# Reading back the diagonal blocks of a triangular inverse in four transfers of 8 rows

## The chip, the cores and the metric

The kernel runs on one core of a Trainium2 chip. The metric is device time in microseconds (us) of one execution, as the median of several runs. Besides that there is one profiled execution, recorded by the hardware profiler; all rows below come from it. Its engines are TensorE (PE for matmuls, PEld for weight loads), VectorE (DVE), ScalarE (ACT), GpSimd (POOL) and SyncE (SP). In this kernel SP issues every DMA. Each engine runs its own list of instructions strictly in order.

## The reference, cut to what matters

A two-layer model on 512 tokens of width 1024. Each layer is a gated feed-forward block, a mixer, and a second feed-forward block. The mixer joins three branches by gates: retention, a sparse attention, and RWKV-7, which is a recurrence over tokens:

```python
def step(S, inp):
    r_t, w_t, k_t, v_t, kk_t, a_t = inp
    sa = jnp.einsum('bhvk,bhk->bhv', S, -kk_t)
    S = S * w_t[:, :, None, :] + sa[..., None] * (kk_t * a_t)[:, :, None, :] + v_t[..., None] * k_t[:, :, None, :]
    return S, jnp.einsum('bhvk,bhk->bhv', S, r_t)
```

## The kernel before

**Staging.** `hybrid` runs, per layer, `ffn`, `mixer`, `ffn`. Nearly all PE time is spent in dense products with float32 weights, written as three passes each (L109, L111, L113, output `psd`). The weights are loaded in 256 KB pieces into `raw` (L54, four buffers), and ACT and DVE split each piece into a rounded part `whi` (L49) and a rest `wlo` (L50), three buffers each.

**The recurrence.** Class `Rwkv` handles the 8 heads as 4 pairs (`p` = 0 to 3 in `pairs`). Time is cut into 8 chunks of 64 tokens. `front2` and `mid` prepare a pair, `chain` walks its 8 chunks, `post` finishes it. Within a chunk the recurrence becomes a product with the inverse of a 64 by 64 unit triangular matrix, and `mid` computes these inverses. So there are 8 runs of `mid` in the program, 4 per layer; below they are called the first to eighth inverse.

**The inverse.** `nb` (tile tag `kh`) holds the strict triangles. Its 32 by 32 diagonal blocks, two per chunk and head, are written to a DRAM buffer `dn` in four DMAs (L480). One DMA then reads `dn` back into the tile `N` (tag `bk`, L481): 128 partitions by 32 rows by 32 numbers, the same 32 blocks copied to four groups of 32 partitions, 512 KB in all. The access pattern's outermost dimension is these four copies. After that, POOL runs a forward substitution over rows `u` = 0 to 30. Each row is two instructions, a product into a scratch tile `E` (L490) and a sum into `X` (tag `cum`, L492). Row `u` of the loop reads row `u` of `N` and nothing else of it. The result goes through DRAM once more: out by `dx<-cum` (L497), back into `mt` (L503). Two rounds of small matmuls (L510, L517) then join the blocks.

**Pacing.** After every fourth row, and after the last, PE gets a tiny matmul that reads `X` (L494, the pace). The program calls `fill` behind each pace to place a counted number of dense matmuls (`FP`, `FD`), so PE has work while POOL runs the next rows. While an inverse is under way, other branches' work is mixed in on POOL: `kd` and `m` of retention (L636, L631), `o` (L700), the softmax scaling `L` of the attention (L862), and `uv` of the chain (L542). A scheduler sets the order on each engine, from its own estimate of when each operand will be there. A changed estimate moves instructions on all engines.

**Waits.** SP reaches the read-back when the four writes to `dn` are done. POOL reaches its first row and waits for the read-back. Everything queued behind on POOL waits too.

Of the kernel before, what the change touches and what calls it, by code (L numbers as in the profile page):

```python
# [232 lines left out]
class Rwkv:  # L233
# [198 lines left out]
    def mid(self, d):  # L432

        nc, K, c = self.nc, self.K, self.cst
        st, bk, v = d["st"], d["bk"], d["v"]
        zo, nb = self.zo, self.t("kh", [P, 8, 64])
        for q in range(2):
            for h in range(2):
                s = slice(64 * h, 64 * h + 64)
# [12 lines left out]
        with self.tc.issue_after(zl.ins):  # L452
# [12 lines left out]
            for h in range(2):  # L465
                o = slice(64 - 64 * h, 128 - 64 * h)
                for par in range(2):
                    src = pv4[64 * par:64 * par + 64, :, h, :]
# [6 lines left out]
        dn = K.dram([4, 8, 32, 32], "dn", 2)  # L475
        N = self.t("bk", [P, 32, 32])
        for h in range(2):
            for b in range(2):
                src = nb[64 * h + 32 * b:64 * h + 32 * b + 32, :, 32 * b:32 * b + 32]
                nc.sync.dma_start(dn[2 * h + b].rearrange("c s t -> s c t"), src)  # L480
        nc.sync.dma_start(N, dn.rearrange("b c s t -> (b c) s t")[None].to_broadcast([4, 32, 32, 32]))  # L481

        X = self.t("cum", [P, 8, 32])
        tmp = self.t("E", [P, 8 * 31])
# [673 lines left out]
```

## Time and profile before

| | us |
|---|---|
| median of 3 runs | 3042.56 (3041.69 to 3042.8) |
| the profiled execution, its own time | 3045.66 |
| span in the profile, first to last instruction | 3043.9 |
| PE busy | 2908.3 (96% of the span) |
| DVE, ACT, POOL busy | 1741.9, 1082.4, 736.7 |

The span is read from the page's first lines. A time taken from a row is a time in the profiled execution, which took 3.1 us more than the median. In a timeline row the first number is the start in us from the span's beginning, the second the length. A bracket at the end says how long the engine stood idle just before and what ended that.

### The profile page before, as it was taken

Reading aid. Unit: us, or ns where it says so; the run is one execution under the profiler, and the core shown is the slowest. Engines: PE = TensorE matmul, PEld = TensorE weight load, DVE = VectorE, ACT = ScalarE, POOL = GpSimd, SP = SyncE. Lnnn points to the kernel's source line nnn. Section 1 sums busy time; section 2 is a strip of 40 time slices with the busy share of each in tenths; the row PEclk is TensorE's granted clock in tenths of the full one; section 3 lists DMA queues with packets and bytes.
Section 4 is the critical chain, followed back from the end, with each engine's and each line's share of the span. In section 5 each row is a group of like instructions: output and inputs, shape, how many; then the busy total and the mean of one; then the engine's idle time right before and its main releaser. Section 6 shows DMA issues by size and latency. Waiting matters only on the chain.

```text
span 3043.9 us, 39972 instructions
## 1 busy us (share of the span) xinstructions
PE 2908.3 (96%) x13968; PEld 2378.0 (78%) x13968; DVE 1741.9 (57%) x3694; ACT 1082.4 (36%) x1900; POOL 736.7 (24%) x1206
## 2 busy tenths in 40 slices
PE   9999999899899999999999999998988999999998
PEld 7888887777777778888888888777777777788886
DVE  5443378949674564444354433888485836644433
ACT  4333343244443233333333333533344432433322
POOL 2110124353433031110011101343534321311100
PEclk9999999999999999999999999999999999999999
DMA  4333322122324442333323334221323244423332
GB/s 137 97 97 104 112 92 73 63 88 81 94 84 148 131 153 94 97 97 95 100 94 97 97 107 118 83 71 60 95 74 97 92 143 132 145 94 97 97 97 87
DMA packets 198970, 305.66 MB, mean 100 GB/s; under 512 B 45808, under 2 KB 59888, under 8 KB 198768
## 3 DMA queue, kind: packets, MB, share of 16 engines
q1 hardware_dynamic: 198768, 303.10, 32.7%
q8 instruction: 110, 1.80, 0.3%
q14 instruction: 92, 0.75, 0.1%
HBM read 273.66 MB, written 29.36 MB: 100 GB/s over the span
## 4 chain that ended last, share of the span: by engine, by line
PE 73%; DVE 10%; POOL 7%; DMA 6%; issue 3%; ACT 1%; SPq 0%; DVEq 0%; POOLq 0%; ACTq 0%
PE psd L109 22%; PE psd L113 22%; PE psd L111 22%; POOL cum L492 3%; POOL E L490 2%; DMA bk<-dn 2%; DVE wlo L50 2%; DMA dx<-cum 1%; PE psr L444 1%; PE psr L533 1%; DMA th<-th 1%; PE psf L96 1%; DMA y<-y 1%; PE psr L558 1%; PE psr L96 1%
## 5 line engine op out<-in xcount | busy, mean ns | idle before, releaser
L49 ACT ACTIVATE whi<-raw 128x512 fp32r<-128x512 f32 (+2 forms) x920 | 571.3, 622 | 1300.8 <-PE psd L111 1002.6
L50 DVE TENSOR_TENSOR wlo<-raw,whi 128x512 fp32r<-128x512 f32 (+2 forms) x920 | 646.3, 703 | 552.7 <-ACT whi L49 545.4
L109 PE MATMUL psd<-xh,whi 128*128 128x512 f32 x2144 | 853.5, 398 | 1.5 <-DVE g L203 1.5
L111 PE MATMUL psd<-xl,whi 128*128 128x512 f32 x2144 | 848.9, 396 | 2.2 <-DVE xl L161 2.2
L113 PE MATMUL psd<-xh,wlo 128*128 128x512 f32 x2144 | 849.2, 396 | 0.1
L111 PEld LDWEIGHTS psd<-xl,whi 128*128 128x128 f32 x2144 | 408.1, 190 | 87.2 <-DVE xl L161 4.3
L113 PEld LDWEIGHTS psd<-xh,wlo 128*128 128x128 f32 x2144 | 408.0, 190 | 84.8 <-issue 0.7
L109 PEld LDWEIGHTS psd<-xh,whi 128*128 128x128 f32 x2144 | 408.5, 191 | 83.3 <-DVE g L203 1.7
L207 POOL TENSOR_TENSOR u<-s,u 128x512 f32<-128x512 f32 x88 | 140.9, 1602 | 841.6 <-DVE u L206 745.3
L109 PE MATMUL psd<-ah,whi 128*128 128x512 f32 x704 | 277.4, 394 | 0.0
L113 PE MATMUL psd<-ah,wlo 128*128 128x512 f32 x704 | 276.0, 392 | 0.0
L111 PE MATMUL psd<-al,whi 128*128 128x512 f32 x704 | 273.2, 388 | 0.0
L172 POOL TENSOR_TENSOR sq<-sq,sq 128x512 f32<-128x512 f32 x42 | 56.4, 1342 | 466.0 <-ACT sq L170 466.0
L111 PE MATMUL psd<-wlo,xh 128*128 128x512 f32 (+1 forms) x384 | 159.2, 415 | 0.0
L113 PEld LDWEIGHTS psd<-ah,wlo 128*128 128x128 f32 x704 | 132.1, 188 | 31.0
L111 PEld LDWEIGHTS psd<-al,whi 128*128 128x128 f32 x704 | 132.2, 188 | 29.6
L113 PE MATMUL psd<-whi,xl 128*128 128x512 f32 (+1 forms) x384 | 154.8, 404 | 0.0
L109 PEld LDWEIGHTS psd<-ah,whi 128*128 128x128 f32 x704 | 132.3, 188 | 26.3
L50 DVE TENSOR_TENSOR al<-u,ah 128x512 fp32r<-128x512 f32 x88 | 61.8, 702 | 153.6 <-ACT ah L49 153.6
L109 PE MATMUL psd<-whi,xh 128*128 128x512 f32 (+1 forms) x384 | 149.7, 410 | 0.0
L206 DVE TENSOR_TENSOR u<-psd,rb 128x512 f32<-128x512 f32 x88 | 60.9, 692 | 127.6 <-PE psd L113 127.6
L49 ACT ACTIVATE ah<-u 128x512 fp32r<-128x512 f32 x88 | 55.6, 632 | 169.4 <-POOL u L207 169.2
(305 smaller groups left out, 3946.6 us busy)
## 6 DMA issues: line engine op xcount, KB each, us to landing
raw<-in_wf_dram SPq DMA_DIRECT2D x184, 256.0 KB, 2.6
raw<-in_ffa_in_dram SPq DMA_DIRECT2D x176, 256.0 KB, 2.6
raw<-in_ffb_in_dram SPq DMA_DIRECT2D x176, 256.0 KB, 2.6
th<-th SPq DMA_DIRECT2D x96, 256.0 KB, 3.3
raw<-in_ffa_out_dram SPq DMA_DIRECT2D x80, 256.0 KB, 2.7
raw<-in_wt_dram SPq DMA_DIRECT2D x80, 256.0 KB, 2.8
raw<-in_ffb_out_dram SPq DMA_DIRECT2D x80, 256.0 KB, 2.6
x<-x SPq DMA_DIRECT2D x32, 256.0 KB, 4.4
```

Of the source, the lines that this page charges most:

```text
L49: self.nc.scalar.activation(hi, x, AF.Copy)
L50: self.nc.vector.tensor_tensor(out=lo, in0=x, in1=hi.bitcast(F32), op=ALU.subtract)
L96: return self.nc.tensor.transpose(out, x, self.ident)
L109: nc.tensor.matmul(out, ah, bh, start=start, stop=False)
L111: nc.tensor.matmul(out, ah, bl, start=False, stop=False)
L113: nc.tensor.matmul(out, al, bh, start=False, stop=stop)
L172: nc.gpsimd.tensor_tensor(out=sq, in0=sq, in1=self.ssq[0], op=ALU.add)
L206: nc.vector.tensor_tensor(out=u, in0=pu, in1=self.rb, op=ALU.mult)
L207: nc.gpsimd.tensor_tensor(out=u, in0=s, in1=u, op=ALU.mult)
L444: zl = nc.tensor.matmul(z[:, i * P:(i + 1) * P], bk[s, ck, :], st[h][s, ck, :], start=True, stop=True)
L490: nc.gpsimd.tensor_tensor(out=tv, in0=X[:, 0:n, u:u + 1].to_broadcast([P, n, w]), in1=N[:, u:u + 1, u + 1:].to_broadcast([P, n, w]), op=AL ...
L492: nc.gpsimd.tensor_tensor(out=X[:, 0:n, u + 1:], in0=X[:, 0:n, u + 1:], in1=tv, op=ALU.add)
```

## The change

The one read-back of 32 rows becomes four read-backs of 8 rows each. They read the same `dn`, write the same `N`, and keep the four copies outermost. Each moves 128 KB, a 1 KB piece per partition instead of one of 4 KB. The program issues them in order of `u`.

```diff
-        nc.sync.dma_start(N, dn.rearrange("b c s t -> (b c) s t")[None].to_broadcast([4, 32, 32, 32]))
+        for u in range(0, 32, 8):
+            src = dn.rearrange("b c s t -> (b c) s t")[:, u:u + 8, :]
+            nc.sync.dma_start(N[:, u:u + 8, :], src[None].to_broadcast([4, 32, 8, 32]))
```

The line numbers behind it grow by two, so L490 becomes L492. The built programs differ beyond the four DMAs, because the scheduler now expects the first rows earlier. At each place the order before is shown first, and then the order now. A bracket `[waits ...]` names what an instruction waits for; `DMAHW0` to `DMAHW7` are the eight counters that DMAs take in turn.

POOL, layer 0, first inverse. `E`, `cum`, `bk` belong to the inverse, `kd`, `m` to retention, `uv` to the chain. Before:

```order
L636 TENSOR_TENSOR kd_3824<-X_4091,kdec 128x128 [waits DVE_49]
L631 TENSOR_TENSOR m_4101<-X_4099,rss 128x4x32 [waits Activation_49,Pool_49]
L631 TENSOR_TENSOR m_4101<-X_4099,rss 128x4x32
L490 TENSOR_TENSOR E_4328<-cum_4327,bk_4321 128x31 [waits DMAHW7_49,DMAHW5_49]
L542 COPY uv_4835<-sv_989_4251 64x64 [waits Activation_49,Pool_49]
L542 COPY uv_4885<-sv_989_4251 64x64 [waits Activation_49]
L542 COPY uv_4835<-sv_990_4252 64x64 [waits Activation_49]
L492 TENSOR_TENSOR cum_4327<-cum_4327,E_4328 128x31 [waits Pool_49]
L542 COPY uv_4885<-sv_990_4252 64x64 [waits Activation_49]
L636 TENSOR_TENSOR kd_3824<-X_4099,kdec 128x128 [waits DVE_49]
```

Now:

```order
L492 TENSOR_TENSOR E_4331<-cum_4330,bk_4321 128x31 [waits DMAHW7_49,DMAHW5_49]
L494 TENSOR_TENSOR cum_4330<-cum_4330,E_4331 128x31 [waits Pool_49]
L638 TENSOR_TENSOR kd_3824<-X_4091,kdec 128x128 [waits DVE_49]
L633 TENSOR_TENSOR m_4101<-X_4099,rss 128x4x32 [waits Activation_49]
L492 TENSOR_TENSOR E_4331<-cum_4330,bk_4321 128x30 [waits Pool_49]
L633 TENSOR_TENSOR m_4101<-X_4099,rss 128x4x32
L544 COPY uv_4838<-sv_989_4251 64x64 [waits Activation_49,Pool_49]
L544 COPY uv_4888<-sv_989_4251 64x64 [waits Activation_49]
L494 TENSOR_TENSOR cum_4330<-cum_4330,E_4331 128x30 [waits Pool_49]
L544 COPY uv_4838<-sv_990_4252 64x64 [waits Activation_49]
L544 COPY uv_4888<-sv_990_4252 64x64 [waits Activation_49]
L492 TENSOR_TENSOR E_4331<-cum_4330,bk_4321 128x29 [waits Pool_49]
```

The first row of the inverse moved ahead of one `kd` and one pair of `m`, which now stand behind it.

POOL, same inverse, at rows 7 and 8 of the loop. Before:

```order
L490 TENSOR_TENSOR E_4328<-cum_4327,bk_4321 128x48 [waits Pool_49]
L492 TENSOR_TENSOR cum_4327<-cum_4327,E_4328 128x2x24 [waits Pool_49]
L490 TENSOR_TENSOR E_4328<-cum_4327,bk_4321 128x69 [waits Pool_49]
L492 TENSOR_TENSOR cum_4327<-cum_4327,E_4328 128x3x23 [waits Pool_49]
L490 TENSOR_TENSOR E_4328<-cum_4327,bk_4321 128x66 [waits Pool_49]
```

Now:

```order
L492 TENSOR_TENSOR E_4331<-cum_4330,bk_4321 128x48 [waits Pool_49]
L494 TENSOR_TENSOR cum_4330<-cum_4330,E_4331 128x2x24 [waits Pool_49]
L492 TENSOR_TENSOR E_4331<-cum_4330,bk_4321 128x69 [waits DMAHW0_49,Pool_49]
L494 TENSOR_TENSOR cum_4330<-cum_4330,E_4331 128x3x23 [waits Pool_49]
L492 TENSOR_TENSOR E_4331<-cum_4330,bk_4321 128x66 [waits Pool_49]
```

No instruction moved here. Row 8 (`128x69`) got a wait of its own on the second transfer's counter; rows 16 and 24 got the like.

SP, layer 0, second inverse: the writes to `dn`, the read-back, weight loads (`raw`) and two stores of the retention's output (`y<-sT`). Before:

```order
L54 DMA raw_5679<-in_wt_dram 128x512
L480 DMA dn_5797<-kh_5614 32x8x32 x4
L54 DMA raw_5705<-in_wt_dram 128x512
L481 DMA bk_5798<-dn_5797 128x1x1024
L54 DMA raw_5752<-in_wt_dram 128x512
L54 DMA raw_5770<-in_wt_dram 128x512
L978 DMA y_4_654_3052<-sT_5199 128x512
L978 DMA y_5_655_3053<-sT_5208 128x512
```

Now:

```order
L54 DMA raw_5682<-in_wt_dram 128x512
L480 DMA dn_5800<-kh_5617 32x8x32 x2
L54 DMA raw_5708<-in_wt_dram 128x512
L54 DMA raw_5755<-in_wt_dram 128x512
L480 DMA dn_5800<-kh_5617 32x8x32 x2
L54 DMA raw_5773<-in_wt_dram 128x512
L980 DMA y_4_654_3052<-sT_5202 128x512
L483 DMA bk_5801<-dn_5800 128x1x256 x4
L980 DMA y_5_655_3053<-sT_5211 128x512
```

Here two more weight loads and one store stand ahead of the read-back. On SP the read-back keeps its neighbours at the seven other inverses.

## Rows read from the trace of the kernel before

**Rows 1.** The page's first part: the span, then busy time, share of the span and instructions of each engine.

```profile
span 3043.9 us, 39972 instructions
PE 2908.3 (96%) x13968; PEld 2378.0 (78%) x13968; DVE 1741.9 (57%) x3694; ACT 1082.4 (36%) x1900; POOL 736.7 (24%) x1206
```

**Rows 2.** Who waited for whom over the whole program: total us, times, longest us.

```profile
POOL E L490 <- DMA bk<-dn: 98.4, 8, 28.6
...
PE psr L494 <- POOL cum L492: 24.8, 20, 5.7
...
PE psr L510 <- DVE m L504: 12.0, 14, 2.4
```

**Rows 3.** PE's timeline at the eight inverses: the first PE instruction that waited for POOL in each (start, length, ..., in the bracket the idle time before it and what ended it).

```profile
476.51 0.70 PE L652 MATMUL psf<-X,kd 128*64 128x128 f32 x4 [3.25 <-POOL kd L636]
...
631.45 0.33 PE L652 MATMUL psf<-X,kd 128*64 128x128 f32 x2 [0.52 <-POOL kd L636]
...
802.42 0.38 PE L494 MATMUL psr<-cum,ident 128*128 128x1 f32 x2 [4.69 <-POOL cum L492]
...
946.64 0.38 PE L494 MATMUL psr<-cum,ident 128*128 128x1 f32 x2 [1.98 <-POOL cum L492]
...
1980.88 0.48 PE L652 MATMUL psf<-X,kd 128*64 128x128 f32 x2 [3.10 <-POOL kd L636]
...
2143.44 0.38 PE L494 MATMUL psr<-cum,ident 128*128 128x1 f32 x2 [2.54 <-POOL cum L492]
...
2311.93 0.37 PE L494 MATMUL psr<-cum,ident 128*128 128x1 f32 x1 [5.75 <-POOL cum L492]
...
2457.40 0.38 PE L494 MATMUL psr<-cum,ident 128*128 128x1 f32 x2 [3.38 <-POOL cum L492]
```

**Rows 4.** Busy time in the 7 us that follow each of the longer waits of rows 3 (the window, its length, then us and instructions of PE, PEld, DVE, ACT and POOL, PE's granted clock, DMA share, GB/s).

```profile
476.51:483.51 7.00, 7.00 (x23) 5.42 (x24) 6.10 (x20) 1.78 (x4) 5.98 (x18) 0.60 0.12 37
802.42:809.42 7.00, 7.00 (x27) 5.88 (x28) 1.84 (x6) 1.18 (x3) 5.64 (x18) 0.76 0.00 1
...
1980.88:1987.88 7.00, 7.00 (x28) 5.53 (x29) 6.10 (x20) 2.17 (x5) 5.98 (x18) 0.78 0.10 37
2143.44:2150.44 7.00, 7.00 (x28) 5.70 (x29) 0.81 (x2) 1.86 (x3) 5.91 (x16) 0.76 0.12 39
2311.93:2318.93 7.00, 7.00 (x21) 5.95 (x22) 1.15 (x4) 1.01 (x2) 5.64 (x18) 0.53 0.00 0
2457.40:2464.40 7.00, 7.00 (x26) 5.67 (x27) 1.43 (x3) 1.27 (x3) 5.64 (x18) 0.76 0.13 37
```

**Rows 5.** The chain of work that ended last, in order of time (start, us, what): the read-backs on it, from issue to POOL's release, and after the first of them one transfer of 128 KB out of SBUF (`dx<-cum`) that also has four groups outermost.

```profile
463.96 10.62 DMA bk<-dn
...
504.43 4.74 DMA dx<-cum
...
787.42 11.21 DMA bk<-dn
...
933.47 9.19 DMA bk<-dn
...
1968.48 10.46 DMA bk<-dn
...
2129.74 10.81 DMA bk<-dn
...
2296.36 11.78 DMA bk<-dn
...
2443.83 10.07 DMA bk<-dn
```

**Rows 6.** POOL's timeline at the first, second and sixth inverse.

```profile
474.72 0.24 POOL L490 TENSOR_TENSOR E<-cum,bk 128x31 f32<-128x31 f32 x1 [7.05 <-DMA bk<-dn]
...
476.07 0.39 POOL L636 TENSOR_TENSOR kd<-X,kdec 128x128 f32<-128x128 f32 x1
476.43 0.86 POOL L631 TENSOR_TENSOR m<-X,rss 128x128 f32<-128x128 f32 x2
...
627.30 0.24 POOL L490 TENSOR_TENSOR E<-cum,bk 128x31 f32<-128x31 f32 x1 [4.97 <-DMA bk<-dn]
...
2140.69 0.24 POOL L490 TENSOR_TENSOR E<-cum,bk 128x31 f32<-128x31 f32 x1 [5.62 <-DMA bk<-dn]
```

**Rows 7.** SP's timeline at the first and second inverse: when the read-back, the weight load behind it and the store were issued (the length is that of the issue).

```profile
463.96 0.68 SPq L481 DMA_DIRECT2D bk<-dn  x1
464.75 0.38 SPq L54 DMA_DIRECT2D raw<-in_wt_dram  x1
...
617.22 0.55 SPq L481 DMA_DIRECT2D bk<-dn  x1
...
624.71 0.33 SPq L978 DMA_DIRECT2D y<-sT  x1
```

**Rows 8.** DMA issues: KB each and median us from issue to landing. The first row is of the whole program (a constant of 1 KB per partition), the second of the stretch 463 to 480 us alone.

```profile
cum<-in_idg_dram SPq DMA_DIRECT2D x8, 128.0 KB, 2.0
...
raw<-in_wt_dram SPq DMA_DIRECT2D x2, 256.0 KB, 10.3
```

**Rows 9.** Busy time, clock, DMA share of the 16 engines and GB/s (columns as in rows 4) in two us in which the read-back of the first inverse was under way; and ACT's timeline at the split of the weights that were loaded right behind it (the piece issued at 464.75).

```profile
468.00:470.00 2.00, 2.00 (x11) 1.64 (x10) 2.00 (x7) 0.73 (x2) 0.00 (x0) 1.00 0.25 72
...
484.28 0.63 ACT L49 ACTIVATE whi<-raw 128x512 fp32r<-128x512 f32 x1 [1.06 <-PE psd L113]
```

## The prediction

> **What bounds the kernel now.** I read the page's first part, then the waits, then PE's timeline. PE is busy for 2908.3 of 3043.9 us [rows 1], so time can only be saved where PE stands idle or runs at its lower clock. The table of waits leads to the place: POOL stood 98.4 us, eight times, before the first row of an inverse until the read-back landed, and PE stood 24.8 us at the paces that POOL releases [rows 2]. Most of POOL's 98.4 us costs nothing, because PE had other work meanwhile. What counts is PE's own idle time. In all eight inverses the first PE instruction that waited for POOL stands shortly after the read-back's landing, and the idle times before it are 3.25, 0.52, 4.69, 1.98, 3.10, 2.54, 5.75 and 3.38 us, 25.2 us in all [rows 3]. In the first and fifth the wait is for `kd`, which is queued on POOL behind the inverse's first row; in six inverses it is at a pace or again at `kd`.
>
> A second loss follows the idle time. In the 7 us after it the granted clock was 0.60, 0.76, 0.78, 0.76, 0.53 and 0.76 of full speed in six of the eight inverses, although PE was busy throughout [rows 4]. So a part of each stretch ran at the lower of the two levels (1.2 instead of 2.4 GHz). The work lost is 7 us times one minus the clock: 2.8, 1.7, 1.5, 1.7, 3.3 and 1.7 us, 12.7 us in all. I count none for the second and fourth inverse.
>
> Idle time and clock loss together are what PE can win back, inverse by inverse: 6.05, 0.5, 6.4, 2.0, 4.6, 4.2, 9.05 and 5.1 us. I call these the stakes. Their sum is 37.9 us.
>
> **When the first 8 rows land.** The read-back took 9.19 to 11.78 us from issue to POOL's release [rows 5]. While the first was under way alone, the DMA share was 0.25 and the rate 72 GB/s [rows 9]. That is four engines of 16, and at 72 GB/s the 512 KB take 7.3 us. A transfer of 128 KB that also has four groups outermost took 4.74 us [rows 5]. From 4.74 at 128 KB to 10.62 at 512 KB is 5.9 us for 393,000 bytes, or 67 GB/s, close to the 72. So I read a fixed part of about 3 us and a part that grows with the bytes. The first quarter should land 4.7 us after its issue. The bounds are 2.0 us, the landing of a 128 KB constant with the same 1 KB per partition [rows 8], and 10.6 us, no earlier than the whole. I take 4.7 because that row has the same size and the same outermost dimension. The later quarters follow at the queue's rate and are not waited for: POOL needs 3.4 to 3.8 us or more for the rows of each quarter (14 to 16 instructions, of which the first took 0.24 us [rows 6]), against some 2 us of transfer.
>
> The Trainium skill, "DMA: Bandwidth & Descriptors", section "Anatomy of one DMA", gives each DMA about 2.0 us of fixed cost plus its bytes at 436 GB/s. By that 128 KB would take 2.3 us, all stakes would be won, and the sum would be 37.9 us. The same page's rules advise joining small transfers, which speaks against this change, and by the same formula the whole read-back would take only 3.2 us. The trace has 10.62.
>
> **The change part by part.** *The earlier first row.* Without anything else, POOL's first row would start 10.62 less 4.7, or 5.9 us earlier in the first inverse. From the other rows of rows 5 it is 6.5, 4.5, 5.8, 6.1, 7.1 and 5.4 us in the third to eighth.
>
> *POOL's order.* In the first and fifth inverse one `kd` (0.39 us) and two `m` (0.86 us) that ran before the first row now run after it [rows 6]. They must still be done before the first pace, so 1.3 us of the lead are lost: 4.6 and 4.5 us remain. In the sixth, `kd` and `m` also fall behind the first row, which leaves 4.8; POOL is free for it early enough, as it had waited 5.62 us there [rows 6].
>
> *What PE gets.* PE gains the smaller of stake and lead. First inverse 4.6 (of 6.05), third 6.4 (the stake), fourth 2.0 (the stake), fifth 4.5 (of 4.6), sixth 4.2 (the stake), seventh 7.1 (of 9.05), eighth 5.1 (the stake). The sum is 33.9 us. Where the lead is the smaller, POOL is the next to be late: its 31 rows then set the pace from the first to the last.
>
> *The second inverse* I put at zero. Its stake is 0.5, and SP now reaches the read-back only behind a store. That store was issued at 624.71, the read-back at 617.22 [rows 7]. At worst the quarter lands at 624.7 plus 4.7, so the first row comes 2.1 us later than at 627.30 [rows 6]. At best the store comes earlier too, and the lead covers the stake.
>
> *Three more issues on SP.* At 0.55 to 0.68 us each [rows 7] they hold the queue for about 2.0 us. The next weight load stands behind them. It was issued at 464.75 and landed 10.3 us later [rows 7, 8], at 475.05, so it was itself held by the read-back's bytes, which stay the same. ACT splits this piece at 484.28 [rows 9]. The margin of 9.2 us falls to 4.6 as PE comes earlier, and still covers 2.0. Cost zero; without that cover it would be 2.0 us per inverse.
>
> *Everything else that moved.* Some hundred instructions change places with neighbours, mostly in layer 0 between the first and second inverse. They compute the same and PE stays the bound. I have no row for their sum, and bound it by the one class of waits that lies behind each inverse, PE waiting at L510 for the returned inverse: 12.0 us in all [rows 2]. I allow half of it, 6 us, either way, and take zero, because leads and delays can both come of it.
>
> **The sum.** The profiled execution took 3045.66 us, and 33.9 less is 3011.8. It ran 3.1 us above the median of the runs, so against the median of 3042.56 the forecast is 3008.7, about 3009 us, 1.1% faster. With the first quarter at 2.0 us all stakes are won: 3004.7. With the 6 us either way, 2999 to 3015.
>
> **The rivals.** *First: a transfer's time is mostly fixed, so a quarter lands not much before the whole.* If it takes 7.7 us, each lead shrinks by 3.0, and the gains are 1.6, 0, 3.5, 1.5, 1.5, 1.8, 4.1 and 2.4, or 16.4 us: 3026 us. The 2.0 us of rows 8 speak against it; for it speaks that no row shows a read of this shape at this size. The Trainium skill's fixed cost, in the page and section named above, is of this kind: 2.0 of the 2.3 us it gives a quarter. Chance 0.13.
>
> *Second: the four transfers share the four engines and land together, and the kernel is slower.* Then the first row waits for all 512 KB and for three issues more, 2.0 us longer than now. In the first and fifth inverse `kd` and `m`, which now stand behind that row, come 1.3 us later still. That is 2.0 us in six inverses and 3.3 in two, 18.6 us: about 3061 us. It turns into a loss where the first quarter lands later than some 9.3 us after its issue. Against it: the weight load issued 0.8 us behind the read-back landed at 475.05, after POOL was released at 474.58 (463.96 plus 10.62) [rows 5, 7, 8]. A load that shared the engines evenly with a transfer twice its size would have been done before. The queue seems to serve in order. Chance 0.07.
>
> *Third: the lead is won at the first row and lost by the last.* POOL's rows share their engine with `L`, `o`, `kd` of other branches. If these now fall between rows, the paces wait instead of the first row, and half the gain goes: 3026 us. For it speaks that the 24.8 us at the paces came in 20 waits, so late rows do reach PE [rows 2]. Against it, that 18.3 of these 24.8 us are the first paces of five inverses [rows 3]. Chance 0.08.
>
> That the rows still wait for all four transfers is ruled out by the built order: the first row waits for one counter, and row 8 for another.
>
> **How the numbers follow.** Forecast 0.72, first rival 0.13, third 0.08, second 0.07. The range is 2999 to 3027: it takes in the early landing, the 6 us of moved instructions and both cases at 3026, and leaves out the slower case and the late end of the first rival. A measurement of this kernel can tell about 0.2% (6 us) from no change. Faster by more than that: the forecast, the third rival and most of the first, 0.91. Within: the late end of the first, 0.03. Slower: 0.06.
>
> **What would show it.** In the profile of the changed kernel POOL's wait before an inverse's first row should shrink by about 6 us each, by 40 to 48 us in all from 98.4. The waits of rows 3 should be gone but for a few tenths in the first, fifth and seventh inverse, and the clock in the 7 us after those places near 1.00. PE's busy time should fall by the clock's 12 us. The first quarter's landing, issue to POOL's release, should be 4 to 5 us. If it is over 9, the second rival holds; if it is 7 to 9, the first. If it is under 5 and the time still above 3020, the third holds, and PE's idle time at later paces and at L510 will have grown.

## The result and the profile after

The changed kernel takes 3020.03 us (median of 4 runs) against 3042.68 before. The ratio is 0.9916, with a 95% interval of 0.9895 to 0.9936. So it is faster, by 22.7 us where 33.9 were forecast. The time lies inside the range, 11 us above the forecast. The profiled execution took 3020.28 us, 25.4 less than the one of before. One execution of a later run of this kernel (run 10) took 4052.2 us at a mean granted clock of 0.65 instead of 0.98; it is in no ratio.

The page's first part after the change (columns as in [rows 1]):

```profile
span 3018.5 us, 40018 instructions
...
PE 2901.2 (96%) x13968; PEld 2372.9 (79%) x13968; DVE 1744.9 (58%) x3694; ACT 1081.2 (36%) x1900; POOL 737.7 (24%) x1206
```

PE's busy time fell by 7.1 us and its idle time (span less busy) by 18.3, from 135.6 to 117.3. The waits that answer to [rows 2]:

```profile
POOL E L492 <- DMA bk<-dn: 56.8, 6, 23.9
...
PE psr L535 <- DVE sv L558: 23.9, 25, 3.3
...
PE psr L512 <- DVE m L506: 11.9, 8, 2.9
PE psr L496 <- POOL cum L494: 11.9, 18, 1.2
```

POOL's wait is booked for six inverses only. The other two are booked under `issue`: 3.01 us in the third inverse (its bracket is below) and 2.91 in the seventh. Eight waits of 62.7 us stand against eight of 98.4. PE's waits at the paces halved, and none is longer than 1.2 us. PE's wait at L512 (the former L510) didn't shrink in sum, and its longest grew. One wait grew: at L535 PE waits for `sv`, the state that `chain` hands on from chunk to chunk. Before (L533) it was:

```profile
PE psr L533 <- DVE sv L556: 17.8, 24, 1.8
```

That is 6.1 us more, nearly all of it between the first and second and between the fifth and sixth read-back.

SP's issue of the four read-backs and POOL's first row in the first, second, third and sixth inverse (they answer to [rows 6, 7]):

```profile
462.31 2.35 SPq L483 DMA_DIRECT2D bk<-dn  x4
466.56 0.24 POOL L492 TENSOR_TENSOR E<-cum,bk 128x31 f32<-128x31 f32 x1 [2.98 <-DMA bk<-dn]
...
620.27 2.50 SPq L483 DMA_DIRECT2D bk<-dn  x4
625.71 0.24 POOL L492 TENSOR_TENSOR E<-cum,bk 128x31 f32<-128x31 f32 x1 [1.67 <-DMA bk<-dn]
...
782.45 2.27 SPq L483 DMA_DIRECT2D bk<-dn  x4
787.93 0.24 POOL L492 TENSOR_TENSOR E<-cum,bk 128x31 f32<-128x31 f32 x1 [3.01 <-issue]
...
2117.21 2.31 SPq L483 DMA_DIRECT2D bk<-dn  x4
2123.87 0.24 POOL L492 TENSOR_TENSOR E<-cum,bk 128x31 f32<-128x31 f32 x1 [2.88 <-DMA bk<-dn]
```

From issue to first row it is 4.25, 5.44, 5.48 and 6.66 us, and 4.3 to 5.4 in the other four, 5.2 on average. Before it was 9.3 to 11.9. So the first quarter lands about as forecast. The clock, too, is full in the windows below, in the first, third and fourth inverse (columns as in [rows 4]; in the fourth it hadn't dropped before):

```profile
470.00:477.00 7.00, 7.00 (x36) 5.38 (x35) 6.54 (x23) 2.59 (x6) 6.21 (x19) 1.00 0.27 90
...
802.00:809.00 7.00, 6.48 (x34) 5.48 (x34) 4.34 (x9) 3.37 (x7) 6.16 (x15) 1.00 0.21 71
946.00:953.00 7.00, 6.49 (x30) 4.84 (x30) 1.99 (x3) 1.90 (x4) 5.67 (x18) 1.00 0.29 97
```

It isn't full everywhere. In the sixth inverse PE still waits 1.24 us at a pace, and the clock from the read-back's issue to the first matmul on the returned inverse fell further, first before, then changed:

```profile
2129.74:2176.38 46.64, 42.16 (x213) 33.32 (x211) 15.84 (x36) 14.38 (x27) 32.89 (x93) 0.96 0.27 79
```

```profile
2117.21:2161.87 44.66, 43.07 (x213) 34.01 (x211) 16.44 (x37) 15.28 (x28) 32.05 (x92) 0.92 0.30 84
```

The mechanism is there, and a third of its worth is missing. PE's timeline shows a first suspect, the wait for the returned inverse at L512, in the second, third, fourth and eighth inverse:

```profile
663.08 0.69 PE L512 MATMUL psr<-m,kh 32*32 32x32 f32 x16 [2.02 <-DVE rr L150]
...
824.70 0.69 PE L512 MATMUL psr<-m,kh 32*32 32x32 f32 x16 [2.27 <-DVE m L506]
...
962.90 1.33 PE L512 MATMUL psr<-m,kh 32*32 32x32 f32 x21 [2.76 <-DVE m L506]
...
2457.79 1.77 PE L512 MATMUL psr<-m,kh 32*32 32x32 f32 x32 [2.87 <-DVE m L506]
```

The 7.1 us behind the third of these waits, in the fourth inverse (columns as in [rows 4]):

```profile
962.90:970.00 7.10, 7.09 (x49) 5.98 (x50) 3.45 (x7) 2.02 (x4) 0.00 (x0) 0.57 0.58 189
```

Before, the waits at the fourth and eighth were 1.14 us each, and the clock behind the fourth was 1.00:

```profile
976.21:983.21 7.00, 6.68 (x64) 5.42 (x65) 4.70 (x8) 3.17 (x6) 0.00 (x0) 1.00 0.62 195
```

Now PE idles 2.76 us there and then runs at 0.57, which loses 7.1 x 0.43 = 3.1 us more. Behind the eighth the clock was 0.76 before and is 0.55 now.

### The profile page after: what moved, and what is told of

Same layout as the page of the kernel before. It is cut to its first block, busy times and chain, and to the rows that moved or that the text cites. A ratio compares the mean times of both kernels' runs of the same rounds, so it can differ in the third digit from the quotient of the medians.

```text
span 3018.5 us, 40018 instructions
## 1 busy us (share of the span) xinstructions
PE 2901.2 (96%) x13968; PEld 2372.9 (79%) x13968; DVE 1744.9 (58%) x3694; ACT 1081.2 (36%) x1900; POOL 737.7 (24%) x1206
## 4 chain that ended last, share of the span: by engine, by line
PE 74%; DVE 10%; POOL 7%; DMA 4%; issue 3%; ACT 1%; SPq 0%; DVEq 0%; POOLq 0%; ACTq 0%
PE psd L109 23%; PE psd L113 22%; PE psd L111 22%; POOL cum L494 3%; POOL E L492 3%; DVE wlo L50 2%; DMA dx<-cum 1%; DMA bk<-dn 1%; PE psr L444 1%; DVE X L818 1%; PE psr L535 1%; DMA th<-th 1%; PE psr L96 1%; PE psf L96 1%; DVE m L817 1%
```

## The experiments

**Theories.** The first: the gain is the early landing, and the missing 11 us were eaten by the scheduler's new order of instructions, which the prediction had priced at zero. The rivals: the landing is not what paid (the order or the small transfers did), or the lead was really lost on POOL's later rows. A stage, below, runs from one read-back's issue to the next, the eighth to the program's end.

**1. The four transfers in reverse.**

```diff
-        for u in range(0, 32, 8):
+        for u in (24, 16, 8, 0):
```

> The four transfers of 8 rows are issued in reverse, rows 24 to 31 first, so the inverse's first row waits for the last one. Bytes, count and issues are those of the changed kernel. Theory (the gain is the early landing of rows 0 to 7, and the queue serves the transfers in order): the first row starts 10.5 to 13 us after the first issue instead of 4.2 to 5.5, POOL's wait at the first row is back near 98 us or above it, and the time is 3040 to 3060 us. Rival (the gain comes from the other order of instructions that the scheduler chose, or from small transfers as such): 3018 to 3030 us.

Measured: 3043.61 us, ratio 0.9999 (0.9985 to 1.0012). All of the gain is gone. POOL's wait is 80.5 us in seven inverses and 4.24 in the first, less than the 98 that I expected. Its first row in the first and third inverse:

```profile
462.50 2.35 SPq L483 DMA_DIRECT2D bk<-dn  x4
471.65 0.24 POOL L492 TENSOR_TENSOR E<-cum,bk 128x31 f32<-128x31 f32 x1 [4.24 <-issue]
...
788.85 2.23 SPq L483 DMA_DIRECT2D bk<-dn  x4
799.04 0.24 POOL L492 TENSOR_TENSOR E<-cum,bk 128x31 f32<-128x31 f32 x1 [5.01 <-DMA bk<-dn]
```

The first row comes 9.15 and 10.19 us after the issue, and 10.0 on average of the eight. That is a little earlier than I expected, and no later than with one transfer (10.7 on average). So the last of four transfers lands no later than the one. As the piece that is issued first lands after 4.3 to 6.7 us in the changed kernel, the order of service is the order of issue.

**2. Four transfers by copies.** Each transfer is one of the four copies, all 32 rows.

```diff
-        for u in range(0, 32, 8):
-            src = dn.rearrange("b c s t -> (b c) s t")[:, u:u + 8, :]
-            nc.sync.dma_start(N[:, u:u + 8, :], src[None].to_broadcast([4, 32, 8, 32]))
+        for g in range(4):
+            nc.sync.dma_start(N[32 * g:32 * g + 32], dn.rearrange("b c s t -> (b c) s t"))
```

> Four transfers again, but each is one of the four copies with all 32 rows (128 KB, 32 blocks outermost) instead of 8 rows of all four copies. PE, DVE and ACT keep the order of the kernel before, instruction by instruction. The first row needs all four. Theory (the old read-back is slow because four copies outermost keep it on four of 16 DMA engines, and PE is paid for the landing, whatever the order): the whole tile is there 4 to 6 us after the first issue, the DMA share goes well above 0.25 and the time is 3012 to 3026 us. First rival (what counts is that a part lands before the whole): the first row 10 us after the issue, 3040 to 3046 us. Second rival (the changed order of instructions made the gain): the landing is early and the time still above 3035 us.

Measured: 3010.14 us, ratio 0.9887 (0.9865 to 0.9908), 2 us below the expected interval. SP's and POOL's timeline in the first inverse, then a window of 3 us in which the read-back is under way:

```profile
464.74 1.71 SPq L482 DMA_DIRECT2D bk<-dn  x4
469.17 0.49 POOL L491 TENSOR_TENSOR E<-cum,bk 128x31 f32<-128x31 f32 x1 [0.17 <-POOL uv L543]
```

```profile
465.74:468.74 3.00, 3.00 (x17) 2.48 (x16) 2.93 (x10) 2.90 (x8) 1.73 (x5) 1.00 0.87 244
```

The DMA share is 0.87 at 244 GB/s, where it was 0.25 at 72 [rows 9]. All 512 KB are there when the changed kernel has only its first quarter: the first row starts 4.3 to 5.6 us after the issue in all eight inverses. That fits the Trainium skill, "DMA: Bandwidth & Descriptors", section "Rules for kernel authors", by which an outermost broadcast over c copies, with c below 16, confines a transfer to at most c engines. The trace agrees: 0.25 is four of 16.

The control matters more. PE, DVE and ACT have the order of before, and the landing of the first row is that of the changed kernel. This gives 33.5 us against the kernel before as it was timed beside it (3043.6); 33.9 were forecast for the landing. The changed kernel, with its own order, gets 22.7.

**3. Partitions side by side.** Partition 4 x block + copy; the constant `idg` is laid out to match.

```diff
-            nc.sync.dma_start(N[:, u:u + 8, :], src[None].to_broadcast([4, 32, 8, 32]))
+            nc.sync.dma_start(N[:, u:u + 8, :], src[:, None].to_broadcast([32, 4, 8, 32]))
...
-        nc.sync.dma_start(dx.rearrange("b c (i g) t -> g (b c) i t", g=4), X)
+        for g in range(4):
+            nc.sync.dma_start(dx.rearrange("b c (i g) t -> g (b c) i t", g=4)[g], X[g::4])
```

> The changed kernel with another order of POOL's partitions: the four copies of a block lie side by side (partition 4 x block + copy), so each of the four read-backs has 32 outermost instead of 4, and the result goes out in four writes with 32 outermost instead of one with 4. Theory (chain from issue over first row and 31 rows to the returned inverse sets the time): the first row starts 2.8 to 3.8 us after the issue instead of 4.2 to 5.5, each of the eight chains is 1 to 2 us shorter, and the time is 3006 to 3016 us. Rival (the start of the first row no longer decides, since PE's waits are now elsewhere): 3017 to 3023 us.

Measured: 2993.06 us, ratio 0.9826 (0.9804 to 0.9847), better than expected. The first row starts 2.8 to 4.2 us after the issue. But not all of the gain is the landing's. With four writes of the result the scheduler also puts more work ahead of L512 (20 to 28 dense matmuls instead of 15 to 17 in pairs 1 to 3), and PE waits at most 1.0 us there. Run 9 takes this part alone.

**4. L512 held back.** The transfers are those of the changed kernel. `hist` lists the dense matmuls in the order in which the program makes them, and L512 may not be placed before one of them, counted back from the last for each pair. At -80 this asks for nothing new.

```diff
+HOLD = -80, -50, -20, -58
...
-        for a in (0, 64):
-            for ck in range(8):
-                mm = nc.tensor.matmul(pc[a + 32:a + 64, ck * 32:ck * 32 + 32], nb[a:a + 32, ck, 32:64], m1[a:a + 32, ck, :],
-                                      start=True, stop=True)
+        with self.K.tc.issue_after(K.hist[HOLD[d["p"]]].ins):
+            for a in (0, 64):
+                for ck in range(8):
+                    mm = nc.tensor.matmul(pc[a + 32:a + 64, ck * 32:ck * 32 + 32], nb[a:a + 32, ck, 32:64], m1[a:a + 32, ck, :],
+                                          start=True, stop=True)
```

> The changed kernel, but the first matmuls on the returned inverse (L512) may not be placed before a given dense matmul, so 25, 26 and 29 dense matmuls instead of 16, 15 and 17 stand between the last pace and L512 in pairs 1, 2 and 3. Nothing else is asked of the order. Theory (the forecast's missing part sits at L512, where PE waits 2.0 to 2.9 us in five inverses and then runs 7 us at a lower clock, because dense work stands behind it): these waits fall below 0.6 us and the time is 3004 to 3013 us. Rival (the work is only moved, and the next wait grows by as much): 3017 to 3023 us.

Measured: 3010.54 us, ratio 0.9883 (0.9863 to 0.9903). PE's timeline at the fourth inverse's L512 (L511 here), then the window behind it:

```profile
960.88 1.09 PE L511 MATMUL psr<-m,kh 32*32 32x32 f32 x32
```

```profile
960.90:968.00 7.10, 7.10 (x89) 5.95 (x88) 3.67 (x7) 3.80 (x7) 0.00 (x0) 1.00 0.59 178
```

PE doesn't wait for the returned inverse in any of the eight, and the clock here is 1.00 instead of 0.57. With the same four transfers, order alone is worth 9.5 us. But this isn't the order of before: the pairs 1, 2 and 3 (second to fourth inverse of a layer) now have 25, 26 and 29 dense matmuls between the last pace and L512, where the kernel before has 17 or 18, 14 and 24. And PE gains idle time alone: it idles 108.8 us instead of 117.3 and is busy for 2900.2 instead of 2901.2. So this run takes away waits that the kernel before had too.

**5 and 6. By copies in some pairs only**, to see where the order costs. Run 5 has `(3,)`, run 6 `(0, 1)`.

```diff
-        nc.sync.dma_start(N, dn.rearrange("b c s t -> (b c) s t")[None].to_broadcast([4, 32, 32, 32]))
+        one = dn.rearrange("b c s t -> (b c) s t")
+        for u in range(0, 32, 8):
+            if d["p"] in (3,):
+                nc.sync.dma_start(N[4 * u:4 * u + 32], one)
+            else:
+                nc.sync.dma_start(N[:, u:u + 8, :], one[:, u:u + 8, :][None].to_broadcast([4, 32, 8, 32]))
```

> The changed kernel, but the last pair of each layer (fourth and eighth inverse) reads back by copies, as in e2_by_copies. The first row starts as early either way; the order of instructions differs from the changed kernel's in these two stages alone, where it is that of the kernel before (24 instead of 17 dense matmuls between the last pace and L512). Theory (with the same landing, the changed order costs 4.4 us in the fourth stage and 2.8 us in the eighth): 3011 to 3015 us, and PE's wait at L512 in the fourth and eighth inverse near 1.2 instead of 2.8 us. Rival (the order costs nothing, the difference between e2_by_copies and the changed kernel is the later rows' landing or scatter of the runs): 3017 to 3023 us.

> The changed kernel, but pairs 0 and 1 (first, second, fifth and sixth inverse) read back by copies; the order in these stages is then the one of the kernel before, in the others the changed one. Theory (in layer 0 the changed order costs 9.6 us in the first two stages, in layer 1 nothing): 3008 to 3013 us, the gain over the changed kernel all in the stages of the first two inverses. Rival (order costs nothing): 3017 to 3023 us.

Measured: 3013.68 us, ratio 0.9900 (0.9883 to 0.9917), and 3014.47 us, ratio 0.9903 (0.9887 to 0.9919). The changed kernel has 0.9916 and, run again, 0.9919. The two parts take 0.0016 to 0.0019 and 0.0013 to 0.0016, together about the 0.0029 to 0.0032 of run 2. Neither part is clear of the intervals by itself. In run 5 the wait at the fourth inverse fell from 2.76 to

```profile
964.38 0.66 PE L515 MATMUL psr<-m,kh 32*32 32x32 f32 x16 [1.09 <-DVE m L509]
```

as expected. The split by stages came out less well. In run 5 the eighth stage gained 4.8 us (2.8 expected) and the fourth 0.6 (4.4 expected; 2.1 against the second profile of the changed kernel, run 10). In run 6 the first two stages together took 310.1 us instead of 320.1, as expected. But its time is 1.5 us above the expected interval, and in its profile the stretch behind the eighth inverse's L512 took 565.8 instead of 560.7 us, with the same order. I don't know why.

**7. Side by side, one read-back.** The partitions and the four writes of the result are those of run 3.

```diff
-        for u in range(0, 32, 8):
-            src = dn.rearrange("b c s t -> (b c) s t")[:, u:u + 8, :]
-            nc.sync.dma_start(N[:, u:u + 8, :], src[None].to_broadcast([4, 32, 8, 32]))
+        nc.sync.dma_start(N, dn.rearrange("b c s t -> (b c) s t")[:, None].to_broadcast([32, 4, 32, 32]))
```

> The partitions side by side as in e3_lanes, with one read-back of all 512 KB instead of four: 32 outermost, one issue. The result still goes out in four writes. Theory (16 engines bring the whole tile nearly as early as four engines bring a quarter): the first row starts 3.5 to 5 us after the issue and the time is 2990 to 3003 us, so that the split into rows is worth 0 to 10 us once all engines take part. Rival (one large transfer lands late on any number of engines): first row after 8 us or more, 3020 us or more.

Measured: 2988.06 us, ratio 0.9818 (0.98 to 0.9836), 2 us below the expected interval. SP's and POOL's timeline for the one transfer of 512 KB, then a window of 1 us of it:

```profile
463.43 0.62 SPq L481 DMA_DIRECT2D bk<-dn  x1
467.23 0.45 POOL L490 TENSOR_TENSOR E<-cum,bk 128x31 f32<-128x31 f32 x1
```

```profile
465.43:466.43 1.00, 1.00 (x7) 0.83 (x5) 0.97 (x5) 0.95 (x4) 0.55 (x2) 1.00 0.98 389
```

The whole tile is there within 3.8 us in the first inverse, and within 3.8 to 5.6 in all eight, 4.8 on average. That is about as early as the first quarter of the changed kernel (5.2, and 4.9 in its second profile). By the formula of the Trainium skill, "DMA: Bandwidth & Descriptors", section "Anatomy of one DMA", which the prediction set against 10.62 us, the estimate is 3.2 us. The page states this formula for DMAs that GpSimd issues, and here SP issues them all; with all engines the trace comes near it, with four it doesn't. The split into rows is worth nothing that can be measured once all engines take part (run 3: 2993.06).

**8. Run 3 with the hold in pairs 2 and 3** (`HOLD = -80, -80, -21, -55`).

> e3_lanes with the hold of e4_hold in pairs 2 and 3 (25 and 32 instead of 20 and 28 dense matmuls between the last pace and L512). Theory: the waits of 1.00, 0.64, 0.80 and 0.70 us left at L512 fall to a few tenths and the lower clock behind them goes, 3 to 7 us less than e3_lanes: 2986 to 2990 us. Rival (waits under a microsecond cost no clock, and the returned inverse is used later): 2991 to 2996 us.

Measured: 2988.13 us, ratio 0.9812 (0.9793 to 0.9831). One wait of 0.3 us is left, and 5 us fewer than run 3 are as expected, but the intervals of runs 3 and 8 overlap.

**9. The result in four writes alone.**

```diff
-        nc.sync.dma_start(dx.rearrange("b c (i g) t -> g (b c) i t", g=4), X)
+        for g in range(4):
+            nc.sync.dma_start(dx.rearrange("b c (i g) t -> g (b c) i t", g=4)[g], X[32 * g:32 * g + 32])
```

> The changed kernel, whose result (L499) goes out in four writes of 32 partitions, 32 outermost, instead of one with 4 outermost. The read-backs are the changed kernel's. This is the other half of e3_lanes. Theory: the way from the last row to L512 gets 0 to 1 us shorter, and 4 to 5 more dense matmuls stand before L512 in two pairs, which covers about 1 us of its wait: 3008 to 3016 us, so that about a third of the 27 us between e3_lanes and the changed kernel comes from here and two thirds from the read-back. Rival (the way back is bound by other things, and all of e3_lanes' gain is the read-back's): 3017 to 3023 us.

Measured: 3009.82 us, ratio 0.9891 (0.9877 to 0.9904). Some 9 to 10 of the 27 us between run 3 and the changed kernel are from here.

**10. The changed kernel again.**

> The changed kernel once more, for a second profile of it and the scatter of its stages: 3016 to 3024 us. The first two stages again some 10 us longer than by copies; stages 4 and 8 together 3 to 8 us longer, if the order costs what e2_by_copies and e5_last_pair_by_copies put on it.

Measured: 3018.81 us, ratio 0.9919 (0.9904 to 0.9934). The first two stages took 316.6 us, 6.0 more than by copies where some 10 were expected; stages 4 and 8 together took 8.6 more, where 3 to 8 were.

**11 and 12. Towards the best.** Run 11 is run 7 with the hold in pair 2 (`HOLD = -80, -80, -21, -80`). Run 12 is run 2 with the four writes of run 9 and the same hold.

> e7_lanes_one with the hold of e4_hold in pair 2 alone (24 instead of 21 dense matmuls before L512), where the waits of 0.73 and 0.91 us were left. Theory: these two waits go, 2 to 4 us less than e7_lanes_one, 2984 to 2987 us. Rival (within the scatter): 2987 to 2990 us.

> Read-back by copies as in e2_by_copies, partitions in the old order, the result in four writes as in e9_result_in_four, and the hold in pair 2. Theory (side by side partitions matter only through the number of engines, and copies already use all of them): the first row 4.3 to 5.6 us after the issue, the time 2988 to 3000 us, near e7_lanes_one. Rival (the partitions' order itself saves): 3003 to 3010 us.

Measured: 2984.92 us, ratio 0.9812 (0.9798 to 0.9825), and 2991.39 us, ratio 0.9823 (0.9806 to 0.9841). Both times are as expected. In run 12 the first row starts 4.4 to 6.5 us after the issue, in two inverses later than expected. Run 11 has the lowest median, 1.9% below the kernel before and 1.1% below the changed kernel. Against runs 7, 8 and 12 its interval decides nothing.

## Why the prediction was right in its mechanism and too large in its sum

I cut the profiled execution at each read-back's issue and at the first matmul on the returned inverse (L510 before, L512 after). Between these two stands a chain that PE can't shorten: landing, 31 rows on POOL, and some 7 us for the way back (7.0 to 7.2 before, 7.0 to 8.1 after). From there to the next issue is the rest. The sums of eight each, in us:

| | before | changed | changed again | by copies (run 2) | held (run 4) |
|---|---|---|---|---|---|
| start to the first issue | 463.96 | 462.31 | 462.79 | 464.74 | 464.45 |
| eight chains | 375.35 | 335.83 | 332.75 | 334.78 | 345.30 |
| eight rests | 2204.6 | 2220.4 | 2221.3 | 2206.4 | 2199.3 |
| span | 3043.9 | 3018.5 | 3016.8 | 3005.9 | 3009.0 |

The chains got 40 us shorter in the changed kernel and by copies alike. By copies the rests stayed (+1.8). In the changed kernel they grew by 15.8 and 16.7. The windows of the chains say what went there: here the second, fourth and eighth of the changed kernel, with the sum of all eight.

```profile
620.27:663.08 42.81, 39.81 (x213) 31.93 (x210) 15.90 (x34) 15.28 (x28) 31.53 (x91) 1.00 0.30 86
...
924.69:962.90 38.21, 34.85 (x160) 27.77 (x159) 10.63 (x16) 12.40 (x22) 21.35 (x66) 0.99 0.41 121
...
2419.50:2457.79 38.29, 34.09 (x153) 26.16 (x152) 10.59 (x16) 11.53 (x20) 21.22 (x66) 0.99 0.40 116
sum 335.83, PE 310.96 PEld 247.28 DVE 162.51 ACT 124.31 POOL 222.87; mean PE 38.87 PEld 30.91 DVE 20.31 ACT 15.54 POOL 27.86
```

The same stretches by copies:

```profile
611.78:660.20 48.42, 48.04 (x252) 38.83 (x251) 21.48 (x42) 21.50 (x37) 35.84 (x97) 1.00 0.31 92
...
917.83:956.43 38.60, 37.07 (x169) 29.41 (x168) 11.28 (x17) 12.15 (x21) 21.40 (x66) 1.00 0.43 123
...
2409.66:2448.15 38.49, 37.00 (x167) 28.83 (x166) 11.36 (x17) 12.04 (x21) 21.26 (x66) 1.00 0.42 123
sum 334.78, PE 317.56 PEld 255.17 DVE 170.10 ACT 129.84 POOL 227.84; mean PE 39.70 PEld 31.90 DVE 21.26 ACT 16.23 POOL 28.48
```

In the second, PE has 213 matmuls in 42.8 us and idles 3.0 of them; by copies it has 252 in 48.4 and idles 0.4. In the fourth and eighth the chain is as long in both, with 160 and 153 matmuls instead of 169 and 167. So work left these chains. That the scheduler did so because it expected the inverse back earlier is my reading; no run shows it. In the first layer, part of the work now stands ahead of the second read-back, which SP reaches later: from the first inverse's L512 to the second issue PE has 597 matmuls, and 569 by copies.

```profile
506.14:620.27 114.13, 100.49 (x597) 81.50 (x596) 104.92 (x281) 37.76 (x66) 36.16 (x60) 0.96 0.21 65
```

```profile
506.57:611.78 105.21, 94.04 (x569) 76.10 (x570) 98.72 (x272) 33.08 (x58) 32.51 (x53) 0.97 0.23 68
```

The rest is done behind the chains. PE idles in the chains for 24.9 us, against 17.2 by copies. Before, it was 43.3 us.

Run 1 points the same way. Its order isn't that of before either, its chains are 13.6 us shorter in sum (361.8 us), its rests 12.2 longer (2216.8), and its time is that of the kernel before.

Point by point:

- **The first quarter at 4.7 us**: near (4.2 to 5.5 us, once 6.7; 5.2 on average, 4.9 in the second profile).
- **In-order service, three more issues at zero**: right as far as run 1 shows it, where even the last of four lands no later than one whole.
- **Everything else that moved, zero, at most 6 us either way**: this is the step that failed. It costs 9.9 us by the medians of run 2 and the changed kernel. The size is known to several us only, since the intervals of the two ratios overlap at their ends (0.9865 to 0.9908, 0.9895 to 0.9936). The moves aren't mostly between the first and second inverse, as I had read them: between the last pace and L512 stand 31, 16, 15 and 17 dense matmuls in both layers, where it was 26, 17, 14 and 24 before (18 for 17 in layer 1). The bound came from the waits at L510, as if only their sum could change. That sum stayed at 12 us. What is larger than by copies is idle time elsewhere (PE waits 23.9 us for `sv`, by copies 19.3, and 11.9 us at the paces, by copies 5.7), and time at the lower clock: of the 12.6 us between the two profiles 3.8 are idle time and 8.8 are busy time, for the same instructions (4.8 and 6.1 with the second profile of the changed kernel). A stretch of 60 us behind the second inverse shows it, first in the changed kernel, then by copies:

```profile
690.00:750.00 60.00, 52.48 (x253) 41.77 (x252) 52.51 (x166) 26.48 (x60) 18.84 (x30) 0.91 0.24 74
```

```profile
687.20:747.20 60.00, 52.16 (x277) 41.58 (x276) 56.91 (x182) 29.12 (x68) 24.76 (x33) 1.00 0.26 83
```

The changed kernel's second profile has 0.94 there, run 6, with the order of before in this stage, 1.00. The kernel before has 0.97 with that order, so the order isn't all of it.

- **The stakes, 33.9 us**: right in sum when the order is kept (33.5), but not each by each, and so in part by luck. By copies the stages of the third and seventh inverse gained 3.5 and 4.7 us, where 6.4 and 7.1 were forecast, and the stage of the second gained 6.7, where I had put zero. I took the first wait of each inverse as the stake. In the second inverse that was 0.5 us, though PE idled 3.7 us in its chain, and by copies this chain is 4.6 us shorter.
- **1.3 us lost to `kd` and `m` in the first and fifth**: too small. POOL's rows took 29.7 us there before and 32.1 after, 2.4 more, and PE waits 0.4 to 1.1 us at later paces (3.0 us in sum in the first, where a few tenths were forecast).
- **POOL's wait down by 40 to 48 us, PE busy down by 12**: 35.7 and 7.1. The clock rose where the first waits went, but it fell in the sixth chain and behind L512 in the fourth and eighth.
- **The rivals.** The first and second are out: the landing was early, and run 1, which makes the first row wait for all four, gives 3043.6 and not 3061. The third foretold a loss between first row and L512, by waits at later paces and at L510. The time, 3020, is near its 3026, and its sign (a landing under 5 us, a time above 3020) is nearly met. But the paces' waits halved and the sum at L512 stayed, so it isn't the cause. A little of it is there, in the 2.4 us of POOL's rows in the first and fifth.

**What stays open.** Run 2 differs from the changed kernel by more than order, since its queue is free sooner for the loads behind. In stages 3, 5, 6 and 7, where that holds too, it is between 0.9 us slower and 0.2 faster than the changed kernel's first profile. And in the changed kernel's second profile neither ACT nor DVE waits for a weight load anywhere behind the first read-back, which leaves a sooner load nothing to win there. So I count it as nothing, though no run has the order of before with the changed kernel's transfers. Run 4 has the same transfers and shows that order alone can be worth as much, but it gains by other waits, so it is no second measure of the price. How the 10 us split over the stages is known only roughly: two profiles of the changed kernel differ by 3.6 us in the first two stages.

## What to carry to other kernels

Before splitting a transfer so that its first part lands early, see how many DMA engines carry it: with the copies moved out of the outermost dimension, one transfer of all 512 KB landed about as early as the split one's first quarter (4.8 us after the issue, against 5.2 and 4.9). And where a scheduler sets the order from its own estimate, an earlier operand also moves the work that covered the wait, so the forecast must count matmuls in the stretch between issue and use in the built order, before and after, and not only the waits that go.

## What the runs showed of the hardware

- A read-back of 512 KB with four copies outermost ran at a DMA share of 0.25 and 72 GB/s [rows 9, over 2 us]. In four pieces with 32 outermost it ran at 0.87 and 244 GB/s (over 3 us), and as one transfer with 32 outermost at 0.98 and 389 GB/s (over 1 us).
- Four issues of SP took 2.2 to 2.5 us in the changed kernel, and 1.7 to 1.8 us by copies.
- The granted clock was 0.91 and 1.00 in two stretches of 60 us behind the second inverse, in the changed kernel and by copies, with PE busy for 52.5 and 52.2 us. What makes the difference, these runs don't tell.
